# Moving the second layer's modulation vectors out of the first layer's mixers in a two-layer diffusion trunk

## The chip, the cores and the metric

The kernel runs on one core of a Trainium2 chip. The metric is the device time of one execution in microseconds (us), the median of several runs. TensorE (PE) multiplies, VectorE (DVE), ScalarE (ACT) and GpSimd (POOL) do elementwise work, and SyncE (SP) issues nearly all DMA transfers, in one queue that works in order.

## What is computed

Two layers run over 512 latent tokens and 256 context tokens of width 1024. Each layer starts from six modulation vectors per stream (latent and context), which are one product of a conditioning vector with a large matrix. Cut to what matters here:

```python
mod_lat = (silu(c) @ ada_w[l] + ada_b[l])[:, None, :]        # ada_w[l]: 1024 x 6144
mod_ctx = silu(c_ctx) @ ada_w[l] + ada_b[l]
sh1, sc1, g1, sh2, sc2, g2 = jnp.split(mod_lat, 6, axis=-1)
h = rms_norm(x, norm1_g[l]) * (1 + sc1) + sh1                # before the three mixers
y = token_mixer(h, ...)                                      # attention, Mamba-2 SSD, latent attention, gates
x = x + g1 * y                                               # output product
h2 = rms_norm(x, norm2_g[l]) * (1 + sc2) + sh2               # router and experts
x = x + g2 * hierarchical_moe(h2, ...)
```

The modulation vectors depend on `c` and `c_ctx` alone, so they may be made at any time before their first use: shift and scale of the first norm at the layer's start, all the others from the output product on.

## The kernel before

A layer runs through five stages: `norm1` (scaled tokens, transposed), the SSD mixer (`ssd`), differential and latent attention (`diff`, `mla`), the gates and branch products with the output product (`gates`, `merge`, `outproj`), and the experts (`moe`). In the profiled execution the first layer's mixers take about 50 to 900 us, a dense rest of gates and branch products follows to 1125 us, then the output product to 1228 us and the experts to 1574 us. The second layer repeats this from there.

The program is traced by generators. `weave` takes the mains (the mixers' streams) in turn as long as one is ready by its own count of TensorE time, and otherwise a step of the fills, which are the generators in `self.fills`. What is left of the fills when the mixers end runs by itself in `drain`. The traced order gives each instruction its priority; a planner with its own estimate of durations then fixes the order on each engine, and semaphores guard it on the chip. So PE, and SP's DMA queue, work in a fixed order, and an instruction that waits holds up all behind it on its engine.

`ada(l, banks)` makes the vectors in three banks of 2048 columns: bank 0 holds shift and scale of norm1, bank 1 the gate of the mixers and the shift of norm2, bank 2 the scale of norm2 and the experts' gate. A bank is eight k-steps. Each loads four weight tiles of 128 x 512 (L296, 256 KB each, 32 per bank) and makes four matmuls of 32 columns by 512 (`adaps`), each into its own quarter of the PSUM rows. Then the bias is added (L303, `mod`), four transposes (`modT`) and small copies give the feature-major vectors (L311, L313), and for banks 1 and 2 two stores (L319) put rows in DRAM (`modd`). The weight tiles take turns in the six `raw` buffers, which all projection weights (L167 in `wload`) use too.

Before, the first layer's bank 0 is made in its `norm1`. The fill of the first layer's mixers is banks 1 and 2 of layer 0 and then all three banks of layer 1 (L2043), beside a second fill of gates and branch products. The second layer's mixers have only the gates and branch products as fill. Between the layers, `norm1(1)` scales the tokens on DVE (L456), transposes them on PE (`xT`), applies shift and scale in `parts` (`hhi`, `hf`, `hlo`), and `pf_kd` and `pf_xbc` are the first products of the SSD mixer. At the entry to the experts, DVE routes the last two token tiles, `rkp` and `ip` rank them and make lists, an indirect DMA gathers token rows from `h2d` (stored at L1597 and L1605), `xgp` transposes them, and `hp` is the first pair's first product, in the single PSUM bank of the pool `pf`.

Of the kernel before, what the change touches and what calls it, by code (L numbers as in the profile page):

```python
# [11 lines left out]
F32 = mybir.dt.float32  # L12
# [8 lines left out]
S = 512  # L21
# [12 lines left out]
class Te:  # L34
    """TensorE, with a count of the time its work takes."""
# [18 lines left out]
class Trunk:  # L54
# [65 lines left out]
    def rsqrt(self, v, n):  # L120
        """v: [128, n] float32, positive -> a tile of v ** -0.5."""
# [6 lines left out]
        if n == 2:  # L128
            # by column, for fewer steps one after the other
# [21 lines left out]
    def split_to(self, hi, lo, src, eng=None):  # L151
        """src (SBUF or PSUM float32) -> hi, lo (float32r)."""
        nc = self.nc
        nc.scalar.activation(hi, src, AF.Copy)
        (eng or nc.vector).tensor_tensor(lo, src, hi.bitcast(F32), op=OP.subtract)

    def wload(self, src, kk, n, fill=False, both=False):
        """Weights [128, kk, n] in DRAM -> (hi, lo) float32r per k-tile."""
# [19 lines left out]
    def proj_fm(self, w, c0, rhs, segs, name="pf"):  # L178
        """feature-major product: 128 columns from c0 of the units w, over rhs(k, part) -> psum per segment."""
# [22 lines left out]
    def psum(self, single=False):  # L202
        """PSUM's banks but the fills' one: three alone and two pairs, or seven alone."""
# [9 lines left out]
    def setup(self):  # L213
# [35 lines left out]
        # silu(c), silu(c_ctx), features on partitions, each over 16 columns  # L249
        self.cT = self.cp.tile([128, 8, 2, 16], F32, name="cT")  # L250
        self.ss1 = self.cp.tile([128, 2, 6], F32, name="ss1")
        # router: logits, one-hot rows of both choices and their sum, what a slot learns of its token
# [5 lines left out]
        # 128 * tile, lane + 1, 0, and half the weight in three bf16 parts  # L258
# [4 lines left out]
        # 1024 * expert, in the first lane  # L263
# [18 lines left out]
    def ada(self, l, banks=(0, 1, 2)):  # L282
        """mod vectors of layer l: norm1 shift/scale by feature, the other rows to DRAM."""
        nc, a = self.nc, self.a
        P = self.P[l]
        for b in banks:
            acc = self.pss((128, 512), name="adaps")
            ab = self.fp.tile([128, 512], F32, tag="gth", name="adab", bufs=2)
            for q in range(4):
                nc.sync.dma_start(ab[32 * q:32 * q + 32, :],  # L290
                                  a["adab"][l, b, q][None, :].to_broadcast([32, 512]))
            for k in range(8):
# [8 lines left out]
                yield LAT_ADA  # L301
            mod = self.fp.tile([128, 512], F32, tag="gth", name="mod", bufs=2)
# [21 lines left out]
    def params(self, l):  # L324
# [24 lines left out]
        # -exp(A_log)  # L349
# [3 lines left out]
    def prep(self, l):  # L353
        """Tables of layer l that depend on its small parameters."""
# [16 lines left out]
        # lambda  # L371
# [9 lines left out]
        # diff: gain rows of q (scaled by 64 ** -0.5) and k, and with rope folded in  # L381
# [17 lines left out]
        # mla: q nope row carries both gains and 96 ** -0.5; rope tables for q and k  # L399
# [21 lines left out]
    def sumsq(self, t, halves):  # L421
        """sums of squares of a tile's rows, by half."""
# [5 lines left out]
    def norm1(self, l):  # L428
        """norm1 with its scale and shift, feature-major, in two parts: the latents; returned, the context."""
# [30 lines left out]
        else:  # L460
            self.kdw = self.wload(self.a["wh"][l, 0], 8, 128, both=True)
            scale(range(6))
        self.hhi = self.hx.tile([128, 8, T], FR, tag="hx", name="hhi")
# [28 lines left out]
        if l == 0:  # L492
            # transposed while the scale is on its way
# [8 lines left out]
        def part(s, ts, tsl):  # L502
            for k in range(8):
                parts(k, s, tsl, raw[s, k] if (s, k) in raw else flip(k, s, ts))
        part(*segs[0])

        def context():
            if l == 0:
                scale(range(4, 6))
            part(*segs[1])  # L510
        return context
# [8 lines left out]
    def weave(self, mains):  # L520
        """trace the mains side by side, the first that is ready first, and the fills where none is."""
# [26 lines left out]
    def drain(self):  # L548
        """the rest of the fills, by themselves."""
# [7 lines left out]
    def ssd(self, l, last):  # L557
# [12 lines left out]
        def s_dt():  # L570
# [13 lines left out]
            # dt = softplus(raw + bias): max(x, 0) + log1p(exp(-|x|)), the log by its atanh series  # L584
# [18 lines left out]
            # within-chunk sums up to each token (forward) and from it (backward), and chunk totals  # L603
# [67 lines left out]
        def s_state(d):  # L671
            """states before each chunk, in direction d."""
# [27 lines left out]
        def prep(t, g):  # L700
            """decay terms of chunk t, group g."""
# [29 lines left out]
        def ready(t):  # L731
            """both scans have read chunk t's inputs."""
# [100 lines left out]
    def gates(self, l, last):  # L833
        """tanh(gate / 2) of all channels, to DRAM."""
# [5 lines left out]
        # a block's weights come in halves, of 4 k-tiles each; a segment starts with the half that the one before  # L840
        # ended with, so that the other is free for the next block early
# [79 lines left out]
    def diff_qk(self, l, hd, last, QK):  # L921
# [9 lines left out]
        for g2 in range(3):  # L931
# [10 lines left out]
            # the gains, and rope  # L942
# [19 lines left out]
        def norm(g2):  # L962
# [3 lines left out]
            # q as [hi | lo | hi], k as [hi | lo], per component  # L966
# [47 lines left out]
    def flipped(self, out, x, sin, n):  # L1014
        """out = sin times x with the halves of each 2 * n features swapped."""
# [7 lines left out]
    def softmax(self, S, n, name):  # L1023
        """exp(S - max), with the sums; S in PSUM [128, n]."""
# [8 lines left out]
    def pT(self, P, nk):  # L1033
        """transposed probabilities: [128 keys, nk, 128 queries]."""
# [11 lines left out]
    def diff_attn(self, l, hd, qT, kT, V, last):  # L1046
# [42 lines left out]
        def tail():  # L1089
            """norm of the head's outputs, by token; to DRAM."""  # L1090
# [1015 lines left out]
WCOL = 512  # L2106
# [104 lines left out]
```

## Time and profile before

| | us |
|---|---|
| median of 3 runs (2753.17 to 2762.5) | 2756.99 |
| profiled execution, span | 2754.7 |
| PE busy in the span | 2552.6 |
| DVE busy | 1547.1 |
| ACT busy | 947.5 |
| POOL busy | 790.2 |

The profiled execution lies 2.3 us below the median. PE is busy for 93% of the span. Read it by stage: busy shares of other engines matter only where PE waits, and the granted clock says at which of its two levels PE ran.

### The profile page before, as it was taken

Reading aid. Unit: us, or ns where it says so; the run is one execution under the profiler, and the core shown is the slowest. Engines: PE = TensorE matmul, PEld = TensorE weight load, DVE = VectorE, ACT = ScalarE, POOL = GpSimd, SP = SyncE. Lnnn points to the kernel's source line nnn. Section 1 sums busy time; section 2 is a strip of 40 time slices with the busy share of each in tenths; the row PEclk is TensorE's granted clock in tenths of the full one; section 3 lists DMA queues with packets and bytes.
Section 4 is the critical chain, followed back from the end, with each engine's and each line's share of the span. In section 5 each row is a group of like instructions: output and inputs, shape, how many; then the busy total and the mean of one; then the engine's idle time right before and its main releaser. Section 6 shows DMA issues by size and latency. Waiting matters only on the chain. (4 is left out here: it accounts for less than half of the span.)

```text
span 2754.7 us, 40612 instructions
## 1 busy us (share of the span) xinstructions
PE 2552.6 (93%) x15408; PEld 1880.9 (68%) x15408; DVE 1547.1 (56%) x3507; ACT 947.5 (34%) x2041; POOL 790.2 (29%) x687
## 2 busy tenths in 40 slices
PE   6999999989899999978999888998998899969998
PEld 2876677878677888864444477887887677764443
DVE  4785445564655003477777767736465554475555
ACT  4232324444455321341111232334453463331111
POOL 2231421113300136343222133542233212532221
PEclk9999999999999999988999889999999999979999
DMA  7214643313401546658999221132112123879995
GB/s 232 60 52 127 204 135 111 106 62 111 135 34 47 176 155 219 195 193 338 374 361 366 110 80 62 54 104 62 58 56 89 54 81 112 295 240 365 411 410 209
DMA packets 157592, 457.50 MB, mean 166 GB/s; under 512 B 17744, under 2 KB 29808, under 8 KB 132432
## 3 DMA queue, kind: packets, MB, share of 16 engines
q1 hardware_dynamic: 151984, 432.56, 44.2%
q0 software_dynamic: 5120, 20.19, 2.1%
q8 instruction: 123, 2.02, 0.3%
q10 hardware_dynamic: 288, 2.10, 0.2%
q14 instruction: 77, 0.63, 0.1%
HBM read 413.81 MB, written 40.97 MB: 165 GB/s over the span
## 5 line engine op out<-in xcount | busy, mean ns | idle before, releaser
L171 POOL TENSOR_TENSOR wlo<-raw,whi 128x512 fp32r<-128x512 f32 (+1 forms) x298 | 394.4, 1335 | 1052.9 <-ACT whi L170 925.9
L170 ACT ACTIVATE whi<-raw 128x512 fp32r<-128x512 f32 (+1 forms) x348 | 214.2, 625 | 298.9 <-PE pf_g L47 78.5
L1909 DVE TENSOR_TENSOR x<-x,fp 128x512 f32<-128x512 f32 x332 | 208.7, 681 | 69.7 <-PE fp L47 69.6
L47 PE MATMUL pf_g<-hhi,whi 128*128 128x512 f32 (+1 forms) x576 | 217.7, 378 | 11.4 <-ACT gth L866 11.3
L47 PE MATMUL pf_g<-hhi,wlo 128*128 128x512 f32 (+1 forms) x576 | 214.0, 372 | 5.0 <-POOL wlo L171 5.0
L47 PE MATMUL pf_g<-hlo,whi 128*128 128x512 f32 (+1 forms) x576 | 214.3, 372 | 0.0
L1898 POOL TENSOR_SCALAR Sm<-itok,sl 128x768 fp32r<-128x768 f32 (+2 forms) x33 | 63.9, 1937 | 352.7 <-PE fp L47 348.3
L47 PE MATMUL pf_wb<-mo,whi 128*128 128x512 f32 (+1 forms) x576 | 157.8, 361 | 5.7 <-DVE gt L1437 5.6
L47 PE MATMUL fp<-yh,Sm 128*128 128x512 f32 (+1 forms) x332 | 144.6, 436 | 1.7 <-ACT yh L1894 0.8
L47 PEld LDWEIGHTS pf_g<-hhi,whi 128*128 128x128 f32 x576 | 111.9, 194 | 42.5 <-ACT gth L866 17.6
L47 PE MATMUL fp<-yl,Sm 128*128 128x512 f32 (+1 forms) x332 | 132.5, 400 | 0.9 <-DVE yl L1895 0.4
L47 PEld LDWEIGHTS pf_g<-hhi,wlo 128*128 128x128 f32 x576 | 111.4, 193 | 31.1 <-issue 11.1
L47 PEld LDWEIGHTS fp<-yh,Sm 128*128 128x128 f32 (+1 forms) x332 | 62.8, 190 | 93.6 <-issue 44.6
L47 PEld LDWEIGHTS pf_g<-hlo,whi 128*128 128x128 f32 x576 | 111.9, 194 | 20.4 <-issue 7.7
L47 PE MATMUL adaps<-adaw,cT 128*32 128x512 f32 x384 | 107.9, 613 | 16.5 <-DVE n1v L449 10.4
L1866 ACT ACTIVATE hd<-hp 128x256 f32<-128x256 f32 (+1 forms) x33 | 12.7, 384 | 317.7 <-PE hp L47 317.7
L47 PE MATMUL yep<-wd,hdT 128*64 128x512 f32 x520 | 120.6, 599 | 0.8 <-ACT hdT L1878 0.8
L47 PEld LDWEIGHTS pf_wb<-mo,whi 128*128 128x128 f32 x576 | 101.7, 190 | 24.6 <-DVE gt L1437 5.4
L47 PE MATMUL hp<-wgb,xgT 128*64 128x512 f32 x368 | 111.3, 602 | 0.0
L47 PE MATMUL dqk<-whi,hhi 128*128 128x256 f32 x384 | 110.3, 287 | 0.0
L47 PE MATMUL dqk<-whi,hlo 128*128 128x256 f32 x384 | 109.0, 284 | 0.0
L47 PE MATMUL dqk<-wlo,hhi 128*128 128x256 f32 x384 | 109.0, 284 | 0.0
(449 smaller groups left out, 6568.0 us busy)
## 6 DMA issues: line engine op xcount, KB each, us to landing
wd<-in_dn_dram SPq DMA_DIRECT2D x62, 1024.0 KB, 9.1
wga<-in_gu_dram SPq DMA_DIRECT2D x52, 1024.0 KB, 13.0
adaw<-in_adaw_dram SPq DMA_DIRECT2D x192, 256.0 KB, 4.0
wgb<-in_gu_dram SPq DMA_DIRECT2D x44, 1024.0 KB, 13.2
raw<-in_wh_dram SPq DMA_DIRECT2D x120, 256.0 KB, 3.1
wgc<-in_gu_dram SPq DMA_DIRECT2D x27, 1024.0 KB, 16.0
raw<-in_win_dram SPq DMA_DIRECT2D x96, 256.0 KB, 3.5
raw<-in_wo_dram SPq DMA_DIRECT2D x64, 256.0 KB, 5.4
```

Of the source, the lines that this page charges most:

```text
L47: self.te.matmul(out, lhsT, rhs, **kw)
L170: nc.scalar.activation(hi[:, :m], raw[:, :m], AF.Copy)
L171: (nc.vector if both and k0 else nc.gpsimd).tensor_tensor(lo[:, :m], raw[:, :m], hi[:, :m].bitcast(F32), op=OP.subtract)
L1866: nc.scalar.activation(hd, hp[:, :256], AF.Tanh, scale=0.5)
L1898: nc.gpsimd.tensor_scalar(Sm, itok[:m], sl[:, 0:1], None, op0=OP.is_equal)
L1909: nc.vector.tensor_tensor(x2[:, t, cs], x2[:, t, cs], fp, op=OP.add)
```

## The change

Layer 1's three banks leave the fill of the first layer's mixers. Bank 0 becomes a third stream of the first layer's output product, `s_ada`, which may start once the last weights of that product have been asked for; there it accumulates in the pool `pf`, takes its bias after the products, and takes the bias tile from the `raw` buffers too. Bank 1 is stepped by `norm1(1)` between the token blocks of the latents: three k-steps ahead of the first, one ahead of each other. Bank 2 (with what might be left of bank 1) is the first fill of the second layer's mixers. In all places `mod` now takes the place of the bias tile instead of a tile of its own. Comments went too.

```diff
-    def ada(self, l, banks=(0, 1, 2)):
+    def ada(self, l, banks=(0, 1, 2), alone=False):
...
-        for b in banks:
-            acc = self.pss((128, 512), name="adaps")
-            ab = self.fp.tile([128, 512], F32, tag="gth", name="adab", bufs=2)
+
+        def bias(b):
+            if alone:
+                ab = self.wp.tile([128, WCOL], F32, tag="raw", name="adab", bufs=3072 // WCOL)[:, :512]
+            else:
+                ab = self.fp.tile([128, 512], F32, tag="gth", name="adab", bufs=2)
             for q in range(4):
                 nc.sync.dma_start(ab[32 * q:32 * q + 32, :],
                                   a["adab"][l, b, q][None, :].to_broadcast([32, 512]))
+            return ab
+        for b in banks:
+            if alone:
+                acc = self.pf.tile([128, 512], F32, tag="f", name="adaps")
+            else:
+                acc = self.pss((128, 512), name="adaps")
+                ab = bias(b)
...
-                yield LAT_ADA
-            mod = self.fp.tile([128, 512], F32, tag="gth", name="mod", bufs=2)
+                yield 0.0 if alone else LAT_ADA
+            mod = ab = bias(b) if alone else ab
...
     def norm1(self, l):
...
             scale(range(6))
+            bank = self.ada(l, (1,))
...
         def part(s, ts, tsl):
             for k in range(8):
+                if l and s == 0:
+
+                    for _ in range(3 if k == 0 else 1):
+                        next(bank, None)
...
             part(*segs[1])
+        if l:
+            self.fills.append([itertools.chain(bank, self.ada(l, (2,))), 0.0])
         return context
...
     def outproj(self, l, last):
...
                 w = self.wload(self.a["wo"][l, c], 8, 256, both=True)
+                if c == 3 and t2s[-1] == nt // 2 - 1:
+                    fin["w"] = True
...
-        return [s_norm(), s_mm()]
+        def s_ada():
+
+            yield lambda: "w" in fin
+            yield from self.ada(l + 1, (0,), True)
+        return [s_norm(), s_mm()] + ([] if last else [s_ada()])
...
     def build(self, upto=99):
...
-                        self.fills.append([itertools.chain(self.ada(l, (1, 2)), self.ada(l + 1)), 0.0])
+                        self.fills.append([itertools.chain(self.ada(l, (1, 2))), 0.0])
```

## Rows read from the trace of the kernel before

**Rows 1.** The page: span, PE busy, and the modulation weights' DMA issues.

```profile
span 2754.7 us, 40612 instructions
PE 2552.6 (93%) x15408; PEld 1880.9 (68%) x15408; DVE 1547.1 (56%) x3507; ACT 947.5 (34%) x2041; POOL 790.2 (29%) x687
...
adaw<-in_adaw_dram SPq DMA_DIRECT2D x192, 256.0 KB, 4.0
```

**Rows 2.** Windows, PE only: from:to, length, busy (instructions), granted clock, DMA share, GB/s.

```profile
320.00:730.00 410.00, 383.06 (x2488) 0.96 0.36 118
...
1250.00:1560.00 310.00, 307.72 (x1506) 0.99 0.82 323
1574.20:1595.80 21.60, 9.39 (x38) 0.58 0.57 183
...
1860.00:2240.00 380.00, 348.01 (x2219) 0.96 0.20 62
```

**Rows 3.** Windows of the tile adaps alone: PE, PEld and DVE busy, then as above.

```profile
0.00:50.00 50.00, 23.31 (x64) 4.05 (x64) 0.69 (x1) 1.00 0.83 270
200.00:263.00 63.00, 18.71 (x64) 2.66 (x64) 0.12 (x1) 1.00 0.39 121
320.00:442.00 122.00, 17.07 (x56) 2.59 (x56) 0.17 (x1) 0.94 0.42 138
442.00:581.00 139.00, 17.61 (x64) 2.57 (x64) 0.93 (x2) 0.99 0.32 101
581.00:728.00 147.00, 11.64 (x64) 1.66 (x64) 0.96 (x2) 0.96 0.36 119
```

**Rows 4.** Timeline of PE: start, duration, operation, count; 256 us and 672 us.

```profile
256.30 1.04 PE L47 MATMUL adaps<-adaw,cT 128*32 128x512 f32 x2
257.28 0.50 PE L47 MATMUL pf_g<-hlo,whi 128*128 128x512 f32 x1
...
671.89 1.07 PE L47 MATMUL adaps<-adaw,cT 128*32 128x512 f32 x8
672.88 1.50 PE L47 MATMUL oss<-ones,osq 128*128 128x1 f32 x12
```

**Rows 5.** Timeline of SP's DMA queue at the kernel's start: the first layer's bank 0.

```profile
17.48 23.59 SPq L296 DMA_DIRECT2D adaw<-in_adaw_dram  x26
```

**Rows 6.** Timeline of PE at the layers' border; in brackets idle before, and releaser.

```profile
1579.43 0.45 PE L51 MATMUL xT<-cst,xt 128*128 128x128 f32 x1 [5.23 <-DVE xt L456]
...
1588.95 2.82 PE L51 MATMUL xT<-cst,xt 128*128 128x128 f32 x12 [3.62 <-DVE hf L477]
...
1610.19 0.40 PE L47 MATMUL pf_xbc<-hhi,whi 128*128 128x512 f32 x1
```

**Rows 7.** Timeline of SP's DMA queue at the layers' border.

```profile
1572.64 2.01 SPq L167 DMA_DIRECT2D raw<-in_wh_dram  x2
1574.71 11.11 SPq L167 DMA_DIRECT2D raw<-in_win_dram  x8
```

**Rows 8.** Windows of all engines (PE, PEld, DVE, ACT, POOL), clock, DMA share, GB/s.

```profile
1230.00:1240.00 10.00, 0.43 (x10) 0.34 (x9) 9.81 (x47) 2.92 (x8) 4.48 (x7) 0.54 0.56 215
1240.00:1250.00 10.00, 3.27 (x47) 2.82 (x48) 6.01 (x19) 1.02 (x5) 3.44 (x5) 0.50 0.73 264
1250.00:1260.00 10.00, 10.00 (x53) 3.60 (x52) 8.34 (x18) 1.16 (x5) 6.35 (x3) 0.77 0.99 382
...
1580.00:1590.00 10.00, 4.18 (x16) 2.99 (x17) 9.03 (x12) 5.66 (x10) 5.82 (x5) 0.50 0.53 166
```

**Rows 9.** Timeline of PE at the entry to the first layer's experts.

```profile
1238.68 0.19 PE L47 MATMUL rkp<-ohs,onesb 128*128 128x32 bf16 x1 [9.02 <-DVE ohs L1702]
...
1250.71 9.01 PE L47 MATMUL hp<-wga,xgT 128*64 128x512 f32 x32
```

**Rows 10.** Timeline of SP's DMA queue at the entry to the experts.

```profile
1206.69 2.14 SPq L167 DMA_DIRECT2D raw<-in_wo_dram  x4
...
1217.92 8.98 SPq L1642 DMA_DIRECT2D wd<-in_dn_dram  x2
1232.41 0.38 SPq L1597 DMA_DIRECT2D h2d<-h2r  x1
```

**Rows 11.** Waits of SP's queue, 190 to 740 us: total, times, longest.

```profile
SPq L296 <- PE adaps L47: 272.0, 47, 44.8
```

## The prediction

> **What bounds the kernel now.** I read the page first: PE is busy for 2552.6 of 2754.7 us [rows 1], so work that leaves PE in a full stage counts, and work that enters an idle stretch may be free. Next I read the windows of PE stage by stage. The stretch in which layer 1's vectors are made, 320 to 730 us, has 383.06 us of work in 410: 6.6% idle. The second layer's attention has 348.01 in 380, or 8.4% idle; the first layer's experts leave next to nothing [rows 2]. PE's real holes are two. At the layers' border, 1574.2 to 1595.8 us, PE works for 9.39 of 21.6 us [rows 2], because transposes wait for DVE's scaled tokens and for PSUM that DVE empties [rows 6]. At the entry to the experts, 1230 to 1250 us, it works for 3.7 of 20 us, DVE routing meanwhile [rows 8]. Both run at the granted clock of 0.50 to 0.54, the lower of the two levels. The change takes three banks from a full stage and puts two of them at these holes and one into another full stage. So PE's total stays, and the question is how much of a bank fits a hole.
>
> **Part 1: the banks leave the first layer's mixers.** The windows of the tile give the three banks as 17.07, 17.61 and 11.64 us of PE [rows 3]. The first has 56 of its 64 records there; the other eight, at the 17.07 / 56 = 0.3 us of its own records, add 2.4. Sum 48.7 us. The transposes and small copies that end a bank move with it and are left out on both sides. The gates and branch products, which had shared the gaps with the banks, now fill them alone and leave less for the dense rest after the mixers. That is a gain only if they can: layer 1's attention has that fill alone and is 1.8 points more idle, which over 410 us is 7.5 us [rows 2]. Part of those points comes from its smaller set of queries, so I take 4 us, between 0 and 7.5. Part 1 gives -48.7 + 4 = -44.7 us.
>
> **Part 2: bank 2 in the second layer's mixers.** It enters as the first fill, with 32 loads on SP among those of the mixers' own weights. The nearest row is the first layer's bank in the same place, the SSD mixer: 18.71 us [rows 3]. PE is nearly full there, and gates that it displaces come later, where they cost the same. Bounds are 11.6 (the cheapest bank) and 18.7 us; I take 18.7, by the row of the same stage. Its loads share the `raw` buffers with the input weights, as they did in layer 0.
>
> The price of a bank depends on how its weights arrive. Two records, one matmul, hold PE for 0.98 us until the next operation starts (256.30 to 257.28), and eight records, all four quarters of the array, for 0.99 us (671.89 to 672.88) [rows 4]. The four quarters do run side by side, but only when four weight tiles lie ready. *The Trainium skill, "TensorEngine Tiling (Array Packing)", Key Properties, has the tiles operate independently and in parallel; by that, a bank would be eight times the price of one step. The trace agrees for single steps, but its banks cost more.* From rows: 8 x 0.99 = 7.9 us against 11.6 to 23.3 us [rows 3]. What that would do to the time is rival B.
>
> **Part 3: bank 1 at the border.** At the kernel's start a bank runs at the pace of its loads: 26 in 23.59 us [rows 5], 0.91 us each, 29 us for 32, and PE is held for 23.31 us [rows 3]. The border is the nearest case: again norm1, again PE otherwise waiting. PE's hole is 21.6 - 9.39 = 12.2 us [rows 2]. 23.3 - 12.2 = 11.1 us remain. A little returns through the clock: the stretch's own work of 4.18 us in 10 runs at 0.50 [rows 8] and would partly run faster if PE is kept busy; I take 2 us. So +9 us, bounds 0 (all in the hole and the waits behind it) and 23.3 (the loads arrive when the hole is over). On SP the 32 loads stand ahead of the input weights, which now issue at 1574.71 [rows 7]; these move behind them by some 29 us, to about 1604. Their first reader starts at 1610.19 [rows 6], so one landing time (4.0 us, of loads of the same size [rows 1]) and the splits just fit. If that cover goes, it costs up to 29 - (1610 - 1585) = 4 us, inside the bounds.
>
> **Part 4: bank 0 at the entry to the experts.** PE has 16.3 us of hole at 1230 to 1250 [rows 8], and the bank is 18.7 to 23.3. But the path there is not PE: it is routing on DVE, the stores of `h2d`, the gather, then `hp` at 1250.71 [rows 9]. The bank touches it three times. Its `raw` buffers come free only after the last weights of the output product, issued at 1206.69; the down weights at 1217.92 wait for the same room [rows 10]. One landing time of 4.0 us later, at about 1222, PE can take its first steps, an estimate. 29 us of loads (part 3) then end at about 1251. `hp` needs the `pf` bank, hence the whole of bank 0 with its bias, loaded last: a landing time of 4 us more, about 1255. That is 4 us behind 1250.71. And behind the waiting loads on SP stand the stores of `h2d` (1232.41) and the first pair's down weights (1217.92) [rows 10]. I take +4 us for all; bounds 0 (the loads come earlier than I think) and 26 (rival D).
>
> **Sum.** -44.7 + 18.7 + 9 + 4 = -13.0 us. On the profiled span, 2754.7 - 13.0 = 2741.7; the median of the runs is 2.3 us higher, so 2744.0.
>
> **Rivals.**
>
> *B, the banks nearly vanish.* If four weight tiles lie ready at each step, bank 2 costs 7.9 us, and banks 1 and 0 fit their holes. -44.7 + 7.9 = -36.8, with up to 4 at the entry: some 2720 to 2724 us. For it: the single steps of rows 4, and the cheap bank of 11.64 us. Against it: the six `raw` buffers are shared, and the bank in the SSD mixer cost 18.71 us.
>
> *C, a bank that misses its hole.* The border's hole opens at 1574 us, but its longest wait (5.23 us) ends at 1579.43 [rows 6], and a first load issued behind 1574 lands at 1579 or later. If PE's fixed order then lets transposes stand behind matmuls that wait for loads, bank 1 costs all of its 23.3 us: -44.7 + 18.7 + 23.3 + 4 = +1.3, or 2758 us.
>
> *D, slower: the DMA queue at the experts' entry.* The bank is 32 x 256 KB = 8.4 MB. Between 1230 and 1250 us, 215 and 264 GB/s already move, against 382 in the next stretch [rows 8]; that leaves (167 + 118) x 10 us = 2.9 MB. The rest competes with expert weights, and the experts' loop has PE full and DMA at 0.82 [rows 2], so little is made up. 5.5 MB at 382 GB/s are 14 us; if SP waits in between for `raw` buffers while the stores of `h2d` stand behind it, the gather is late by that again. SP does wait in this way: 272 us in all for `adaps` to release its buffers in the first layer, 44.8 at the longest [rows 11]. *The Trainium skill, "DMA: Bandwidth & Descriptors", Anatomy of one DMA, says that semaphore waits are taken on the issuing sequencer before dispatch, which speaks against putting such loads ahead of the path's stores. The trace agrees: the waits of rows 11 are the queue's own.* With a price of 26 us for bank 0 the sum is -44.7 + 18.7 + 9 + 26 = +9, or 2766 us. It is slower than before from a price of 17 us on, and measurably so from 25.
>
> *E, the planner puts a bank elsewhere.* Bank 1's loads may be ordered behind the input weights, and its products then run in the mixers at 18.7 us: -44.7 + 18.7 + 18.7 + 4 = -3.3, 2754 us. The generators fix priorities only, so this can be.
>
> **How the numbers follow.** About 0.3%, 8.3 us, is what a measurement of this kernel can tell from no change; faster then means below 2748.7, slower above 2765.3. My forecast (parts 1 to 4 within some 10 us, 2734 to 2754) has 0.50; of that 0.36 lies below 2748.7 and 0.14 above. B has 0.15, all faster. C has 0.17, of which 0.04 slower. D has 0.13, all slower. E has 0.05, 0.03 of it within 0.3% and 0.02 slower. So faster 0.51, same 0.14 + 0.13 + 0.03 = 0.30, slower 0.04 + 0.13 + 0.02 = 0.19. The range goes from B's dear end, 2720, to just past D, 2768. The likeliest case's own range is 2734 to 2754.
>
> **What would show each step.** Part 1: the output product starts some 45 us earlier (it now starts at about 1125 us), and PE's idle share in the attention stays below 8.4%. If the output product starts less than 35 us earlier, part 1 is wrong: the banks had stood in gaps that nothing else fills. Part 2: a bank of `adaps` in the second layer's mixers, of 12 to 19 us. Part 3: from the last expert sum to the first `pf_xbc` 45 us instead of 36; if 60, C is right. Part 4: from the last `rkp` to `hp` 16 us instead of 12, `hp` waiting for `mod`; if above 28, D. A granted clock above 0.6 in both holes would show PE busy there. The prediction as a whole is wrong if parts 3 and 4 together cost more than 30 us or nothing.

## The result, and the profile after

The changed kernel takes 2779.8 us (median, 2777.3 to 2783.5), against 2758.4 before in the same comparison: a ratio of 1.0077, 95% interval 1.0062 to 1.0092. It is 21 us slower. The prediction was 2744 us and faster.

The page of after says what hardly changed against [rows 1]: the number of instructions, and but for 12 us PE's busy time.

```profile
span 2777.6 us, 40644 instructions
PE 2564.5 (92%) x15408; PEld 1882.3 (68%) x15408; DVE 1544.6 (56%) x3507; ACT 949.4 (34%) x2041; POOL 791.3 (28%) x687
```

Where the time went is read from first and last starts of a few tiles in both traces (us):

| from, to | before | after | difference |
|---|---|---|---|
| start, first `wo` of the first layer | 1124.3 | 1071.2 | -53.1 |
| first `wo`, first `hp` (output product and entry to the experts) | 126.4 | 152.6 | +26.2 |
| of this: last `rkp`, first `hp` | 12.0 | 37.6 | +25.6 |
| first `hp`, last expert sum `fp` | 322.9 | 321.6 | -1.3 |
| last `fp`, first `pf_xbc` (border) | 36.6 | 60.8 | +24.2 |
| first `pf_xbc`, first `wo` of the second layer | 772.3 | 797.9 | +25.6 |
| first `wo` of the second layer, its last `fp` | 364.8 | 366.4 | +1.6 |

The sum is +23.2 against 22.9 between the spans. So the first layer gave back 53 us, and three places took 76.

The windows of PE say what the places took it for (from:to, length, busy and instructions, granted clock, DMA share, GB/s). Before, from the first `wo` to `hp`, from the last `fp` to `pf_xbc` (the border alone), and from the last `fp` to the second layer's `wo`:

```profile
1124.30:1250.70 126.40, 98.95 (x799) 0.87 0.58 197
1573.60:1610.20 36.60, 24.16 (x119) 0.74 0.43 134
1573.60:2382.50 808.90, 739.96 (x4611) 0.95 0.27 88
```

The same three stretches after:

```profile
1071.20:1223.80 152.60, 120.93 (x869) 0.89 0.66 219
1545.40:1606.20 60.80, 47.52 (x166) 0.81 0.68 218
1545.40:2404.10 858.70, 787.54 (x4746) 0.95 0.32 103
```

PE is idle for 126.4 - 98.95 = 27.5 us before and 31.7 after in the first, 12.4 and 13.3 at the border, 68.9 and 71.2 in the last. The holes are as large as they were, and busy time came on top, most of it the banks' own: 22.0 us in the first stretch, 47.6 in the last. The tile `adaps` alone (PE, PEld, DVE busy, clock, DMA, GB/s) shows bank 0 at 21.4 us, bank 1 at 25.3 and bank 2 at 18.7:

```profile
1100.00:1210.00 110.00, 21.44 (x64) 3.79 (x64) 0.69 (x1) 0.90 0.61 194
1545.00:1600.00 55.00, 25.31 (x64) 3.96 (x64) 0.69 (x1) 0.82 0.72 232
1683.00:1790.00 107.00, 18.70 (x64) 2.61 (x64) 0.69 (x1) 0.95 0.40 124
```

**The entry.** DVE's timeline, in brackets the idle time before and its releaser:

```profile
1186.72 0.29 DVE L1744 TENSOR_REDUCE code<-rt 128x4 f32<-128x128 f32 x1
1208.06 0.69 DVE L313 TENSOR_TENSOR adab<-adaps,adab 128x512 f32<-128x512 f32 x1 [21.05 <-DMA adab<-in_adab_dram]
...
1210.26 1.96 DVE L1839 TENSOR_TENSOR eq<-cst,code 128x512 bf16<-128x512 f32 x4
```

The routing's `eq` needs only `code`, done at 1187.0. But the bank's sum (L313) stands ahead of it on DVE and waits for the bank's last products and the bias, so `eq` starts 23 us late. On PE (next fence) the list sums `ip` stand behind the bank's products as well: the last of these end at 1203.5, the sums follow only at 1211.0, and `hp` starts at once when the gathered rows are transposed. Two orders, PE's and DVE's, thus hold the lists back until the bank's end; e_tail below tells how much is DVE's:

```profile
1197.99 5.55 PE L47 MATMUL adaps<-adaw,cT 128*32 128x512 f32 x14 [0.78 <-DMA adaw<-in_adaw_dram]
1208.81 1.11 PE L51 MATMUL modT<-cst,adab 128*128 128x128 f32 x4 [5.26 <-DVE adab L313]
1211.00 0.37 PE L47 MATMUL ip<-info,eq 128*128 128x3 bf16 x8 [1.08 <-DVE eq L1839]
...
1223.79 2.83 PE L47 MATMUL hp<-wga,xgT 128*64 128x512 f32 x6
```

SP's queue shows that rival D's mechanism did not happen: the stores of `h2d` left it at 1180.7, before the routing ended, and half of the loads came behind them.

```profile
1180.72 2.80 SPq L1624 DMA_DIRECT2D h2d<-h2r  x3
1183.62 0.46 SPq L1616 DMA_DIRECT2D h2d<-h2r  x1
1184.17 15.23 SPq L306 DMA_DIRECT2D adaw<-in_adaw_dram  x16
1199.75 1.80 SPq L293 DMA_DIRECT2D adab<-in_adab_dram  x4
```

**The border.** The same picture, on more engines: DVE waits 21 us in front of the bank's sum with two of the latents' eight blocks still to do; the input weights are issued behind 32 us of bank loads, not directly behind the first weights as in [rows 7]; and ACT, in order too, waits 22 us for them.

```profile
1550.09 32.07 SPq L306 DMA_DIRECT2D adaw<-in_adaw_dram  x32
1582.47 2.27 SPq L167 DMA_DIRECT2D raw<-in_win_dram  x4
```
```profile
1587.66 0.69 DVE L313 TENSOR_TENSOR adab<-adaps,adab 128x512 f32<-128x512 f32 x1 [21.04 <-PE adaps L47]
...
1591.22 0.81 DVE L488 TENSOR_SCALAR hf<-xT,a,sh 128x512 f32<-128x512 f32 x1 [1.43 <-ACT hhi L486]
```
```profile
1587.16 0.63 ACT L170 ACTIVATE whi<-raw 128x512 fp32r<-128x512 f32 x1 [22.12 <-DMA raw<-in_win_dram]
```

What ends last is PE's order. The transposes `xT` of those two blocks stand behind all of the bank's products and its `modT`, from about 1566, when DVE had emptied the sixth block, to 1589.31. DVE's next step (`hf`, above) waits for them by way of ACT, so nothing that was ready stood behind the sum on DVE:

```profile
1586.52 1.05 PE L47 MATMUL adaps<-adaw,cT 128*32 128x512 f32 x2 [1.49 <-DMA adaw<-in_adaw_dram]
1588.40 1.12 PE L51 MATMUL modT<-cst,adab 128*128 128x128 f32 x4 [0.84 <-DVE adab L313]
1589.31 1.91 PE L51 MATMUL xT<-cst,xt 128*128 128x128 f32 x8
```

**Theory.** A bank's end waits for its 32 loads, and every engine that it touches works in order. So at the entry and the border the loads' time lands on the path, and PE's hole stays. *The Trainium skill, "DVE: scalar operands, raw-bit mode, write accounting and state across instructions", section 5, calls DVE's queue one in-order queue; the trace agrees, with `eq` ready at 1187.0 and started at 1210.26.* **Rivals:** the DMA system is what is late (D); or the matmuls' time on PE is the price, wherever they stand.

### The profile page after: what moved, and what is told of

It reads as the page before. It is cut to its first block, busy times and chain, and to the rows that moved or that the text cites. A ratio compares the mean times of both kernels' runs of the same rounds, so it can differ in the third digit from the quotient of the medians.

```text
span 2777.6 us, 40644 instructions
## 1 busy us (share of the span) xinstructions
PE 2564.5 (92%) x15408; PEld 1882.3 (68%) x15408; DVE 1544.6 (56%) x3507; ACT 949.4 (34%) x2041; POOL 791.3 (28%) x687
## 5 line engine op out<-in xcount | busy, mean ns | idle before, releaser
L47 PE MATMUL pf_g<-hhi,whi 128*128 128x512 f32 (+1 forms) x576 | 217.9, 378 | 11.6 <-ACT gth L883 11.5
L47 PE MATMUL adaps<-adaw,cT 128*32 128x512 f32 x384 | 124.5, 635 | 28.1 <-DMA adaw<-in_adaw_dram 16.6
L47 PEld LDWEIGHTS pf_g<-hhi,wlo 128*128 128x128 f32 x576 | 111.8, 194 | 23.2 <-issue 5.0
L47 PEld LDWEIGHTS fp<-yh,Sm 128*128 128x128 f32 (+1 forms) x332 | 62.7, 189 | 93.6 <-issue 44.6
## 6 DMA issues: line engine op xcount, KB each, us to landing
wgb<-in_gu_dram SPq DMA_DIRECT2D x44, 1024.0 KB, 11.9
```

The costliest lines, as they stand in the source:

```text
L47: self.te.matmul(out, lhsT, rhs, **kw)
```

## Experiments

Medians are in us; each ratio is to the kernel before on the same chip.

| run | median | ratio | 95% interval |
|---|---|---|---|
| none | 2712.6 | 0.9834 | 0.9813 to 0.9856 |
| b0_only | 2775.2 | 1.0068 | 1.0043 to 1.0093 |
| b1_only | 2770.8 | 1.0046 | 1.0031 to 1.0061 |
| b2_only | 2777.7 | 1.0070 | 1.0048 to 1.0093 |
| e_tail | 2774.2 | 1.0063 | 1.0039 to 1.0086 |
| e_noload | 2754.7 | 0.9992 | 0.9979 to 1.0005 |
| bd_tail | 2764.8 | 1.0021 | 1.0005 to 1.0036 |
| bd_noload | 2758.1 | 0.9999 | 0.9988 to 1.0011 |
| bd_half | 2766.4 | 1.0028 | 1.0016 to 1.0039 |
| order_after | 2781.0 | 1.0078 | 1.0054 to 1.0103 |
| order_late | 2767.4 | 1.0031 | 1.0018 to 1.0044 |
| b2_late | 2778.7 | 1.0067 | 1.0043 to 1.0092 |
| burst_before | 2747.4 | 0.9959 | 0.9944 to 0.9974 |
| burst_late | 2761.0 | 1.0009 | 0.9995 to 1.0022 |
| burst_lat | 2769.6 | 1.0043 | 1.0020 to 1.0066 |

### One part at a time

```diff
 # none, where layer 1 reads layer 0's vectors (b0_only, b1_only, b2_only keep one of the three
 # places, the other banks return to the fill)
-        return [s_norm(), s_mm()] + ([] if last else [s_ada()])
+        return [s_norm(), s_mm()]
-            bank = self.ada(l, (1,))
+            bank = iter(())
-            self.fills.append([itertools.chain(bank, self.ada(l, (2,))), 0.0])
+            self.fills.append([itertools.chain(bank), 0.0])
```

**none.** 

> The second layer's three banks are not made at all: layer 1 takes layer 0's vectors, so part of the computation is left out and the time is what remains without it. Theory: the changed kernel reached its output product 53.1 us earlier than before, and that is the whole price of three banks in the first layer's mixers; so this kernel should take about 2758 - 53 = 2705 us, and all of the change's loss lies where the banks were put. Rival: the prediction's -44.7, which gives 2713. Both the entry (last rkp to hp, 12 us) and the border (last expert sum to first pf_xbc, 36.6 us) should stand as before.

**b0_only.** 

> Only bank 0 is moved, to the output product; banks 1 and 2 stay in the first layer's mixers. Theory (each place has its own price, and they add): a third of 53.1 comes back, -17.7, and the entry costs 26 as in the changed kernel: +8, 2766 us; from the last rkp to hp 37 us instead of 12, DVE idle some 20 us behind mod. Rival (the prediction's part 4, bank 0 costs 4): 2758 - 17.7 + 4 = 2744 us, and rkp to hp 16 us.

**b1_only.** 

> Only bank 1 is moved, to the layers' border. Theory: -17.7 in the first layer's mixers and the border's whole price; the changed kernel lost about 24 there on the way to pf_xbc, and the gates that had run at the border come later, so +6 or a little more, 2764 to 2768 us; from the last expert sum to the first pf_xbc about 60 us instead of 36.6. Rival (part 3, bank 1 half hidden in PE's hole, +9): 2749 us and 45 us at the border.

**b2_only.** 

> Only bank 2 is moved, to the second layer's mixers. Theory: a bank costs the same there as in the first layer's mixers, -17.7 + 18.7: about 2759 us, no change that can be measured; what the changed kernel lost behind the border beyond 18.7 then belongs to bank 1. Rival: the second layer's mixers make a bank dearer, 26.7 as the changed kernel's stages seemed to say: 2767 us.

| us | before | none | b0_only | b1_only | b2_only |
|---|---|---|---|---|---|
| first `wo`, first layer | 1124.3 | 1070.3 | 1109.4 | 1113.7 | 1114.5 |
| last `rkp`, first `hp` | 12.0 | 11.3 | 38.7 | 11.9 | 11.9 |
| last `fp`, first `pf_xbc` | 36.6 | 38.2 | 38.3 | 59.2 | 36.8 |
| last `fp`, first `wo`, second layer | 808.9 | 814.1 | 811.8 | 831.8 | 837.4 |

Each place has its own price, and they add to what the changed kernel showed: 26 us at the entry, 23 at the border, 28 in the second layer's mixers. Each move alone makes the kernel slower. What I had wrong beforehand is the other side. One bank that leaves the first layer's mixers brings the first `wo` forward by 10 to 15 us, not by a third of 53. On PE, `adaps` falls there from 84.6 us to between 70.3 and 70.8, by 14 us whichever bank goes, and to 34.4 with all three gone, by 16.7 us each. That fits [rows 3], where the bank made last held PE for 11.64 us and the two ahead of it for 17 to 18: with one bank fewer, the dear places stay full. The 10 against 15 goes with the granted clock: before the first `wo`, 51.0 us of PE's work ran at 0.50 in the kernel before, 41.7 in b0_only, 58.7 in b1_only and 54.7 in b2_only. No single move paid. Bank 2 is the extreme: it gave back 9.8 us and cost 28.5, of which `adaps` are 18.8 us,

```profile
1599.20:1721.50 122.30, 4.02 (x10) 0.47 (x10) 0.00 (x0) 0.93 0.21 65
1721.50:1848.60 127.10, 14.83 (x54) 2.15 (x54) 0.69 (x1) 0.99 0.39 121
```

and the rest is 5.8 us more of PE time in the other work and 3.9 of idle time (PE's busy time from the last `fp` to `wo` is 764.6 us against 740.0, the idle time 72.8 against 68.9). The 5.8 us go with the granted clock, as a table below shows.

In the kernel none the first `wo` comes 54 us earlier, as in the changed kernel, but the median falls only by 44.6: the second layer, with the same 4611 matmul records, takes 5.2 us more up to `wo` and 5.7 from there to `hp`.

### The entry

```diff
 # e_tail
-                ab = self.wp.tile([128, WCOL], F32, tag="raw", name="adab", bufs=3072 // WCOL)[:, :512]
+                ab = self.mq.tile([128, D], F32, tag="y", name="adab", bufs=1)[:, :512]
...
-                nc.sync.dma_start(ab[32 * q:32 * q + 32, :],
+                (nc.scalar if alone else nc.sync).dma_start(ab[32 * q:32 * q + 32, :],
...
-            yield from self.ada(l + 1, (0,), True)
+            self.rest = self.ada(l + 1, (0,), True)
+            for _ in range(8):
+                yield next(self.rest)
...
         ls = {0: lists(eqs, self.weights)}
+        for _ in self.rest:      # bias sum, transposes, copies
+            pass
 # e_noload
+                    if not alone or (k == 0 and hf == 0):
                         w = self.wp.tile([128, WCOL], F32, tag="raw", name="adaw", bufs=3072 // WCOL)
                         nc.sync.dma_start(w, a["adaw"][l, b, :, k, hf * WCOL:hf * WCOL + WCOL])
```

**e_tail.** 

> As b0_only (only bank 0 moved, 2775 us, last rkp to hp 38.7 us), but the end of the bank (bias sum on DVE, transposes, copies) is issued behind the first token list instead of ahead of the routing, and the bias has room of its own and comes early, by ScalarE's queue. All 32 loads and the matmuls stay where they were. Theory 1, DVE alone: mod holds the routing's one-hot rows for some 21 us; without it rkp to hp falls to about 18 us and the time to 2755. Theory 2, DVE and PE in turn: PE too has the last adaps ahead of the list sums, so the sums come right behind the last adaps (8 us earlier than in b0_only): rkp to hp about 30, 2767 us. Theory 3, the DMA queue (rival D of the prediction: stores, gather and expert weights late): no change, 2775 us.

Theory 2 holds on the stretch it speaks of: 32.5 us instead of 38.7. DVE (first fence, from e_tail) now goes straight on from `code` to `eq`, 0.8 us behind the last `rkp`, where b0_only's `eq` came 24.8 us behind it. But PE has the last bank products ahead of the list sums; paced by their loads they end at about 1248.5, and the sums follow at once (second fence):

```profile
1229.39 0.29 DVE L1746 TENSOR_REDUCE code<-rt 128x4 f32<-128x128 f32 x1
1229.60 1.96 DVE L1841 TENSOR_TENSOR eq<-cst,code 128x512 bf16<-128x512 f32 x4
```
```profile
1246.32 2.25 PE L47 MATMUL adaps<-adaw,cT 128*32 128x512 f32 x6 [0.53 <-DMA adaw<-in_adaw_dram]
1248.51 0.76 PE L47 MATMUL ip<-info,eq 128*128 128x3 bf16 x24
```

So DVE's order, with the late bias, is worth 6.2 of the entry's 26.7 us; the rest hangs on PE's order, though no run put the list sums ahead of the bank's products. The forecast of the whole, 2767 us, failed: the median is 1 us below b0_only's, which by the intervals (some 0.24% each way) can't be told from a gain of 6. In the two profiled executions the first `wo` came at 1114.8 and 1109.4. The first layer's mixers do the same in both, but PE ran 62.1 us of its work there at the granted clock of 0.50 in e_tail and 41.7 us in b0_only.

**e_noload.** 

> As b0_only, but of bank 0's 32 weight loads only the first is made and all matmuls read that tile; the vectors of layer 1's first norm are therefore not the reference's. Matmuls, bias and the rest stay. If what the entry costs is waiting for loads, passed on by engines that work in order (theories 1 and 2), rkp to hp falls to 12 to 16 us and the time to about 2750. If the matmuls and small steps themselves cost it, it stays above 30 us.

Last `rkp` to `hp` takes 15.5 us. The 32 matmuls, the sum and the transposes at the entry cost 3.5 us there; the loads are the rest, 23.2 us of b0_only's 26.7. PE's wait for the gathered rows hardly differs with and without them (5.5 and 5.1 us), so the loads delay the lists' start and not the gather. Yet even then the kernel does not beat before by what can be told: the first `wo` comes 10.9 us earlier, the way from there to `hp` takes 1.7 back and the second layer, up to its `hp`, 4.8.

### The border

```diff
 # bd_tail: eight k-steps as in b1_only, the bank's end to the fills
-                    for _ in range(3 if k == 0 else 1):
+                    for _ in range(min(3 if k == 0 else 1, max(0, 6 - k))):
 # bd_half: four k-steps, the rest to the fills
+                    for _ in range({0: 2, 2: 1, 4: 1}.get(k, 0)):
 # bd_noload: as e_noload, for bank 1 of layer 1
```

**bd_tail.** 

> As b1_only (only bank 1 moved, 2771 us, last expert sum to first pf_xbc 59.2 us), but the end of the bank with its sum on DVE is left to the fills behind the border. Theory 1, DVE's queue: the latents' last two hf and hlo no longer stand behind mod, the border falls to about 40 us, the time to 2752. Theory 2, PE in order and loads ahead of the input weights: the 32 adaps stand on PE ahead of the last xT and pf_kd at the pace of their loads, and the input weights are issued behind the loads; nothing but the 2 us of the transposes is saved, 57 us, 2769.

**bd_noload.** 

> As b1_only, but of bank 1's 32 loads only the first is made and all matmuls read that tile; the second layer's gate of the mixers and shift of the second norm are therefore not the reference's. If the loads' pace is what the border costs, 32 matmuls in groups of four take 8 to 16 us of PE (at the higher and the lower of the two clock levels) beside a hole of 12 us: border 37 to 45 us, 2748 to 2756. If PE's own time were the price, the border would stay above 55 us.

**bd_half.** 

> As bd_tail (border 47.9 us, 2765 us), but only four of bank 1's eight k-steps stand at the border, the other four go to the fills of the second layer's mixers. Theory (after the sum on DVE, the 32 loads ahead of the input weights are what is left): with 16 loads the input weights are issued some 15 us earlier, and the border falls to 38 to 41 us; the four steps cost 9 us in the mixers, so the time stays near 2762. Rival (the matmuls between the transposes): the border falls by half of 11 us, to 42, and the time by less.

bd_tail lies between its theories: 47.9 us, 11.3 less than b1_only. The edit takes the bank's end away, and with it the planner gave PE another order. In b1_only, as in after, eight of the latents' transposes stand on PE behind the whole bank (first line, 1602.06). In bd_tail the latents' last transposes stand between its products (second line), and `pf_kd` too:

```profile
1602.06 1.04 PE L51 MATMUL xT<-cst,xt 128*128 128x128 f32 x8
```
```profile
1581.60 0.65 PE L51 MATMUL xT<-cst,xt 128*128 128x128 f32 x4
```

So the 11.3 us can't be put down to DVE's queue, theory 1: DVE's sum and PE's order moved together. What is left are 11 us, and here is SP's queue in bd_tail, then in bd_half:

```profile
1567.62 36.67 SPq L306 DMA_DIRECT2D adaw<-in_adaw_dram  x32
1605.37 10.10 SPq L167 DMA_DIRECT2D raw<-in_win_dram  x9
```
```profile
1570.79 16.93 SPq L306 DMA_DIRECT2D adaw<-in_adaw_dram  x16
1588.55 9.01 SPq L167 DMA_DIRECT2D raw<-in_win_dram  x8
```

With 16 loads the input weights come 17 us earlier and the border falls to 40.6 us, inside the theory's 38 to 41 and only 1.4 from its rival. So of the border's 22.6 us the place of the bank's end makes 11.3. Loads and matmuls of the bank make the other 11.3, and halving both takes 7.3; how these split is not settled. bd_half's time does not fall: from `pf_xbc` to `wo` its mixers take 784.8 us, 10.6 more than bd_tail's.

bd_noload is the surprise: no loads but one, and the border still takes 45.2 us, 8.6 more than before. Against b1_only the loads' pace is thus 14.0 of the 22.6 us, and the bank's products and end are 8.6 without it. PE runs 24 bank products in a row, 6.97 us, between the first transposes and the others:

```profile
1571.39 2.91 PE L51 MATMUL xT<-cst,xt 128*128 128x128 f32 x12 [6.25 <-DVE xt L467]
1574.23 6.97 PE L47 MATMUL adaps<-adaw,cT 128*32 128x512 f32 x48
1581.13 0.66 PE L51 MATMUL xT<-cst,xt 128*128 128x128 f32 x4
```

PE's hole at the border is no free room: it is one chain, transpose, ACT, DVE, transpose. Whatever PE does in between in its fixed order delays the next transpose, and the hole moves behind it.

### Both repairs in the changed kernel, and bank 2 later

```diff
 # order_after: e_tail and bd_tail in the changed kernel; order_late adds, and b2_late has alone:
-            self.fills.append([itertools.chain(bank, self.ada(l, (2,))), 0.0])
+            self.fills.append([bank, 0.0])
+            self.fills.append([self.ada(l, (2,)), self.te.t + 150.0])
```

**order_after.** 

> The changed kernel with both ends of banks moved out of the way, as in e_tail and bd_tail. Theory (the two stalls by order on DVE and PE add up in the changed kernel as they do alone): the entry falls from 37.6 to about 31.5 us, the stretch from the last expert sum to the second layer's output product by about 10 us, so 2780 - 16 = 2764 us. Rival (what is won there returns as PE work later, as the gates are displaced): 2775 to 2780 us.

**order_late.** 

> As order_after, and bank 2 may start only 150 us (by the kernel's own count of TensorE time) after the second layer's mixers begin, in the attention. Theory: a bank's price is set by how many of its four weight tiles lie ready; in the first layer's attention the third bank cost 11.6 us of TensorE against 18.7 in the state-space mixer, so bank 2 falls from 28.5 us to 16 to 21, and the time to 2752 to 2757, no better than before. Rival: the mixers of the second layer make a bank cost what it does wherever it stands in them: 2764.

**b2_late.** 

> As b2_only (only bank 2 moved, 2778 us, 837.4 us from the last expert sum to the second layer's first wo against 808.9 before), but it may start only 150 us after the mixers begin. Theory (tiles ready): 28.5 us of price fall to 16 to 21, so 2765 to 2770 us. Rival (place does not matter): 2778.

order_after bears out its rival, at 2781.0 us. The entry falls from 37.6 to 34.0 us, not to 31.5, and the border from 60.8 to 49.4, but from the last `fp` to the second layer's `wo` it takes 861.1 us, as before the repair (858.7): PE is idle for 72.2 us instead of 71.2. The theory's additive sum was wrong. order_late gives 13.6 us on top, where its theory had 7 to 12, but from a start 17 us above the theory's: 2767.4, not 2752 to 2757. b2_late, the same edit by itself, gives nothing (2778.7 against 2777.7). What tells the two apart is the granted clock. Its two levels are 0.50 and 1.00 (1.2 and 2.4 GHz), and PE's busy time from the last `fp` to the second layer's `wo` can be taken apart by it:

| us | before | none | b2_only | b2_late | order_after | order_late |
|---|---|---|---|---|---|---|
| PE busy | 740.0 | 744.7 | 764.6 | 766.8 | 788.9 | 778.2 |
| of it `adaps` | 0 | 0 | 18.8 | 15.7 | 41.6 | 36.2 |
| of it at the clock of 0.50 | 46.8 | 57.5 | 60.1 | 69.4 | 61.3 | 48.8 |
| busy, less `adaps`, less half of the time at 0.50 | 716.6 | 715.9 | 715.7 | 716.3 | 716.6 | 717.6 |

The last row takes half of the time at 0.50 as lost to the clock (in bd_noload the same `pf_kd` products start 0.43 us apart at 0.50 and 0.23 at 1.00). It is an estimate, and it differs by 2 us at most. The later place saves 3 to 5 us of `adaps` in both kernels. But order_late did 12.4 us less work at 0.50 than order_after, and b2_late 9.3 us more than b2_only, which ate the saving. The mean clock of whole executions says the same of each run: 0.961 to 0.965 in order_late's ten, 0.959 to 0.961 in order_after's four, 0.955 to 0.956 in b2_late's four against 0.956 to 0.959 in b2_only's. Why the clock is granted less in one order of the work than in another stays open.

What nearly all of these share: over the seventeen kernels PE's idle time from the last `fp` to the second layer's `wo` lies between 63.6 us (bd_half) and 72.8 (b2_only), but for burst_late's 78.5 (below), and the stretch's length follows its busy time.

### What a bank costs by itself

```diff
 # burst_before: the kernel before, in all banks of the first layer's mixers
+                # step(q) is the matmul of a quarter, traced behind each load before, now behind all four
+                lead = step(3)
+                with self.tc.issue_after(lead.ins):     # on PE, behind the quarter that is loaded last
+                    for q in range(3):
+                        step(q)
 # burst_late: order_late with the same; burst_lat: burst_before with
-LAT_QK, LAT_SM, LAT_PT, LAT_ADA, LAT_HD, LAT_MS = 10.0, 6.0, 1.4, 2.6, 6.0, 2.0
+LAT_QK, LAT_SM, LAT_PT, LAT_ADA, LAT_HD, LAT_MS = 10.0, 6.0, 1.4, 8.0, 6.0, 2.0
```

**burst_before.** 

> The kernel before, unmoved banks; but in all banks of the first layer's mixers the four matmuls of a k-step stand together on TensorE, behind the step's last load, instead of singly as each load comes. Theory: two or more of the four quarters then run side by side and a step holds TensorE for about 1 us (eight records in 0.99 us), a bank for 8 instead of 11.6 to 18.7. Of the five banks' 84.6 us some 40 remain; with a third of the gain lost in gaps, 2757 - 30 = 2727 us. Rival: the matmuls had stood in gaps that nothing else fills, or wait for the last load with all work behind them: 2757 or more.

**burst_late.** 

> As order_late (2767 us; banks moved, ends out of the way, bank 2 in the second layer's attention), and the four matmuls of a k-step stand together as in burst_before, in the first layer's banks, at the border and in the second layer's attention. Theory (a bank costs the TensorE time that its matmuls hold): the first layer's two banks give back 16 us, the border's and the attention's 18.4 + 13.8 us fall to about 12 + 9, together 27 us of TensorE; of burst_before's 34 us saved, 11.5 came out of the time, so a like share here gives 9 to 20: 2747 to 2758 us. Rival (order and loads set the price): at the border the step must wait for its last load in front of the transposes, the border grows to over 55 us, and the time stays at 2767.

**burst_lat.** 

> As burst_before (2747 us), but by the kernel's own count a bank's step comes every 8 us of TensorE instead of every 2.6, so that its four loads can land first. Theory (late loads hold the grouped step): the banks in the attention fall from 12.3 and 10.6 us to about 8, and the time by 3 to 5 us more, 2742 to 2744. Rival: the banks then run into the stage behind, where nothing waits, and cost as much: 2747 or more.

burst_before is faster than both kernels: 2747.4 us, 11.5 less than before. In PE's timeline from 180 to 760 us the kernel before has 79 rows of `adaps`, 35 of them a single matmul (x2); burst_before has 47, 36 of them four (x8). Its windows of `adaps`:

```profile
50.00:320.00 270.00, 18.34 (x136) 2.68 (x136) 1.38 (x2) 0.96 0.35 111
320.00:442.00 122.00, 8.51 (x60) 1.25 (x60) 0.67 (x1) 0.94 0.41 134
442.00:581.00 139.00, 12.29 (x60) 1.77 (x60) 0.69 (x1) 0.98 0.34 109
581.00:800.00 219.00, 10.60 (x64) 1.52 (x64) 0.68 (x1) 0.98 0.28 91
```

The first of these windows before:

```profile
50.00:320.00 270.00, 38.28 (x136) 5.56 (x136) 1.37 (x2) 0.96 0.33 104
```

Against these 38.28 and the 17.07, 17.61 and 11.64 us of [rows 3] that is 35 us of PE time, of which 17.7 reach the first `wo` (1106.6). The other half became idle time: PE's idle time up to the first `wo` is 86.3 us instead of 69.1. So the forecast of 2727 us was 20 too low. *The Trainium skill, "TensorEngine Tiling (Array Packing)", Key Properties, lets tiles run in parallel, and has TensorE drained when the tiling mode changes. The first agrees with a bank of 8.5 us; the drain speaks for fewer groups too, but no run separates it.*

burst_late puts the moved banks at 10.05 us (border) and 8.53 (attention), instead of order_late's 22.4 and 13.8 (the 18.4 of the expectation leaves out eight records):

```profile
1540.00:1620.00 80.00, 10.05 (x64) 1.30 (x64) 0.69 (x1) 0.86 0.62 202
1720.00:1850.00 130.00, 8.53 (x64) 1.26 (x64) 0.69 (x1) 0.97 0.42 134
```

It takes 2761.0, 6.3 us less than order_late and no better than before. Of 17.6 us of `adaps` only 4.2 leave the second layer's stretch, since PE's idle time there grows from 67.8 to 78.5 us, and the border grows from 47.8 to 53.3 us, near the rival's 55. So of the PE time that grouping saves, half reached the time in burst_before's first layer, where other work stands by, and a quarter in burst_late's second.

burst_lat's theory failed: at a step every 8 us nearly three banks (184 records) are left for 600 us and later, where they hold PE for 29.7 us, and the first `wo` comes at 1129.3. The rival was right.

## Why the prediction was wrong, point by point

**What bounds the kernel.** That PE's time counts held, and more than I used it. The holes were read rightly in size, and wrongly as room: PE's idle time at the border is 12.4 us before and 13.3 after. Rows 6 and 9 named the releasers (DVE's `xt`, `hf`, `ohs`): a hole whose releaser is a chain through other engines is filled for nothing only if the filler delays no link of the chain.

**Part 1** (-44.7): 53.1 us at the first `wo`. Its two terms were near: `adaps` falls there by 50.3 us, for 48.7, and PE's idle time grows by 5.9, for 4. Mis-sized is what it put at nothing: PE's other work falls by 8.7 us more. The banks' ends, left out on both sides, leave this stretch, and work at the clock of 0.50 falls from 51.0 to 41.9 us, worth some 4.5 us by the estimate above. As a whole, without the banks anywhere, the kernel is 44.6 us faster; that this meets the term so closely is partly chance, since 54 came back and 11 went elsewhere.

**Part 2** (+18.7): `adaps` took 18.7 us as forecast, but the move alone cost 28.5 us. The failed step is "PE is nearly full there, and gates that it displaces come later, where they cost the same": PE's other work took 5.8 us more, with 60.1 us of work at the clock of 0.50 instead of 46.8, and 3.9 us of idle time came with it.

**Part 3** (+9, bounds 0 to 23.3): 24.2 us. The step that failed is 23.3 - 12.2 = 11.1, the bank in the hole: no part of the hole was used. Rival C had place, mechanism and price (60 us at the border, 60.8 measured): in PE's fixed order the transposes stood behind matmuls that waited for loads. The bank itself held PE for 25.3 us, not 23.3. The cover for the input weights held in after, where `pf_xbc` starts 23.7 us behind their issue and without a wait of PE.

**Part 4** (+4, bounds 0 to 26): 26.2 us. The bank's own time was near: the forecast had its bias landing at about 1255, which is 1202.5 in after, where the last `rkp` comes 52.5 us earlier; it was 1208.06. What failed is the overlap. The forecast had routing, lists and gather run beside the bank, with only `hp` behind it. Measured, the list sums start behind the bank's end, at 1211.0, and from them to `hp` it is 12.8 us. I followed the bank through `raw` buffers, the `pf` bank and SP's queue, and never asked what stands behind its products on PE and behind its sum on DVE: both times it was the lists. Rival D's price (26) was met by another mechanism. The stores of `h2d`, which D had behind SP's waits, were out in time.

**The sum.** C and D were priced as alternatives, each with the other's place at its cheap value. They have one cause, loads that pace an engine in order, and came together: with both, the prediction's own terms give -44.7 + 18.7 + 23.3 + 26 = +23.3 us, and 22.9 were measured between the spans. That these meet so closely is luck: Part 1 gave 8.4 us more than its term, and the border and the second layer's mixers took 7.8 more than theirs. Rivals with a common cause need a case in which both come true; with one, 2780 us would have been in view.

**Rival B** was right on the price of a bank whose tiles lie ready (8.5 us) and wrong on this change: nothing in it makes them lie ready. **E** did not happen.

**What would show each step** worked for part 1, for C (a border of 60 us) and for the whole ("wrong if parts 3 and 4 together cost more than 30 us": 50.4). Two signs misled. Above 28 us at the entry was to mean D, and it came without D's mechanism. A clock above 0.6 was to show PE busy in the holes; it was 0.81 at the border and 0.72 from the last `rkp` to `hp`, with holes as large as before.

## What to carry to other kernels

Before moving work into an engine's hole, list for each engine that the work touches what comes behind it in that engine's order, and until when the work's last operand can be late; here PE's list sums stood behind products that were paced by 32 loads, which is most of the entry's 26 us, and a 0.7 us sum on DVE, waiting for the same, added 6. A hole inside a chain across engines is not room, and an idle share that stays the same while work moves is the sign of it. Price what one unit less gives back, not a mean: here one of five banks was worth 10 to 15 us, not 18. Look at the moved work's own cost first, since grouping its steps gained 11 us where moving it lost 21.

## What was not expected of the hardware

In after, the bias of bank 0 (four loads of 64 KB, issued behind 16 of 256 KB) was waited for until 1208.06, 6.5 us after SP had finished issuing it; its loads there take 6.6 us in the median from issue to landing, against 2.1 over the whole kernel before. The large ones ahead of them take 5.3 there: these small loads, at the end of a full queue, were as late as the large ones.

The same matmuls of the second layer's stretch, 4610 or 4611 records, held PE for 740.0 us before, 743.9 in burst_before and 744.7 in none, at a mean granted clock of 0.95 in all three. That mean hides what tells them apart: 46.8, 54.8 and 57.5 us of the work ran at 0.50. Half of the difference, the estimate above, is 4.0 and 5.4 us; measured are 4.0 and 4.7. A few us of difference between two executions are of this kind.
